# Two-layer diffusion trunk on one core: modulation steps placed in other stages, and a new order around the second layer's first tile of seven products

## The chip, the cores and the metric

The kernel runs on one core of one Trainium2 chip. The metric is device time in microseconds (us). Before the change the median of three runs is 1700.57 us (1700.29 to 1706.34).

Five engines of the core work side by side, each with its own list of instructions: TensorE (PE, matrix products, with its weight loads shown as PEld), VectorE (DVE), ScalarE (ACT), GpSimd (POOL) and SyncE (SP, which in this kernel only issues transfers from memory). An engine works through its list in order, so an instruction that waits holds up those behind it on the same engine. Matrix products go to PSUM, everything else lies in SBUF; a buffer is a slot of a named tile, and a new tile of that name waits until the slot is free.

## The reference, cut to what matters

The model is a trunk of two layers for two groups of tokens that share the weights: 512 sample tokens and 128 prompt tokens, D = 1024 features, float32. Every layer does this for each group:

```python
mod = silu(c) @ w_mod[l] + b_mod[l]          # six parts of 1024 for each group
h = rmsnorm(x, norm_mix) * (1 + mod[1]) + mod[0]
x = x + mod[2] * (mixer(h) @ w_out)
h = rmsnorm(x, norm_ffn) * (1 + mod[4]) + mod[3]
u = conv3(h @ w_up) + conv_b                 # 2 * 2816 columns, three taps along the tokens
x = x + mod[5] * ((silu(u[gate]) * u[a]) @ w_down)
```

The mixer of layer 0 is a latent attention of twelve heads (queries through a rank of 384, keys and values through one of 256, with a positional part of 32) beside a mean over windows of several widths. That of layer 1 is a neighbourhood attention and a windowed attention. At the end `x` is normalised once more. The latents, keys and values of the prompt are outputs too.

`w_mod` is the largest weight that has only two vectors to multiply (the `c` of the sample and that of the prompt): 2 x 1024 x 6144 numbers.

## The kernel before

**Columns and precision.** Activations are held transposed: 128 features on the partitions, tokens along the free side. The 512 sample tokens, a column of zero on either side of the prompt and the 128 prompt tokens make 642 columns. They are worked in two halves: `HALF` is 352 and 290 columns, and the second layer's feed-forward uses `EVEN`, twice 322. A float32 factor is split into a high and a low part of a shorter type, and a product is the sum of high times high, high times low and low times high. So every weight tile and every activation needs a split: ACT writes the high part (L117 for weights) and DVE or POOL subtracts it from the source for the low part (L113).

**Modulation steps.** Most of `w_mod` isn't multiplied on PE. A *step* takes one tile of 128 rows and 512 or 256 columns (`mods_of` lists them, L280): it is loaded (`mod_loads`, L289), and for each of the two vectors it is multiplied by one factor per row and added to an accumulator (`mod_step`, L297). The first vector is done by one instruction of DVE (L316), the second by a product on ACT (L313) and an addition on POOL (L314); in the first of eight steps ACT writes both accumulators (L310). After eight steps DVE transposes each accumulator (L325) and reduces it (L326). When a whole part of 1024 columns is complete, `mod_finish` (L331) makes small products on PE (L337) and the bias on DVE. `mods` makes one step and lets `mod_finish` follow five steps later; `mods_until` stops ahead of a named part. How many raw tiles can be in flight is the `ring`; the queue of the loads is ACT's in the first layer's input projections and SP's later.

Before the change the first layer's parts are distributed so: part 2 (the gate of the mixer) as 16 steps of 512 columns in the input projections, part 4 (the scale of the feed-forward) as 32 steps of 256 in the attention, part 3 (the shift) as 16 steps of 512 in the output projection, two behind each of its products (`MODS_OUT`); part 5 and all of the second layer's parts lie in the first feed-forward, with a ring of two.

**Orders written by hand.** In the start, the input projections, the attention units, the second layer's mixer and all of `Mix` the order of the program is the order of each engine (`manual_schedule`). `MLA_IN` (L49) is a list of pieces of the input projections, each a local function of `mla_in` (L556): `p` a product, `zc` its copy, `sq` squares, `nw` the root of the normalisation by Newton steps, `sc` the scaling with the high part, `lo` the low part, `xc` the copy of the pooled half into a padded tile, `xa`, `xb`, `xm` its sums, `m` one modulation step. `MLA_UNITS` (L63) does the same for an attention unit: one head and one half of the tokens, 24 units in all; the second list is for odd units. `m` there works from the third unit on, until `MLA_MODS` steps are done.

**The output projection of layer 0** (`out_proj`, L450) and the first feed-forward are ordered by the framework's planner, from the order of the program, the readiness of operands and the release of slots; so is SP's queue everywhere. In `out_proj` the loop runs over both halves and eight products: `x` and `w_out` of a product are loaded in the iteration that uses them, three raw `w_out` tiles having been fetched before; behind every product stand the residual sum (`add_x`), the squares and two modulation steps. The normalisation of the first half (`normed`) stands behind product 1 of the second half. It makes `nt` (L424), the high part on ACT (L437) and the low part on DVE (L438) of the activation `ha`, which the feed-forward's first product reads.

**The second layer's feed-forward** is the class `Mix` (L1542). `begin` makes the output projection, the squares, the root and the normalised activations. Its loop over the second half's products has behind each product a piece `after[p_]` (splits of weights for the first tiles, loads, normalisation). The first four tiles of `w_up` (`PLAIN = 4`) are plain: four quarter products, `a` and gate, for two halves. From tile 4 on each tile takes seven products of quarters in place of eight (`p1` to `p7`, L1937) of sums of weights (`sums`, on POOL, gives the blocks S1 to S4; L1897) with sums of activations (T1 to T4). The results are put together on DVE: `u2`, `u3`, `c22`, `c21`, `c12` (L1966 is the addition of all of them). `block` (L1909) splits one block of the weights; `load` (L1892) brings one raw tile into a ring of three, two loads ahead. The convolution of the tile before stands between the products: `gid`/`aid` (centre, ACT), `tapg`/`tapa` (two outer taps, DVE, L1997), `silu`, `mul` (L2020), `ghi`/`glo` (the split of the result). `middle` (L1843) makes the plain tile 3 and the blocks of tile 4, and `slot` (L2029) makes one tile of seven products and the parts of `w_down` that go with it; only the first call, for tile 4, gets the convolution of the tile before (`pv`), since a later tile convolves itself.

Of the kernel before, what the change touches and what calls it, by code (L numbers as in the profile page):

```python
# [49 lines left out]
f.xp0 ln.c f.wk f.xp1 nw.c.0 m nw.c.1 p.q0.1 p.q1.0 zc.q0 sq.q0 sc.c.1.0 p.q1.1 sc.c.1.1 lo.c.1.1 sc.c.0.1 r.wk p.q2.0 sc.c.0.0 rc  # L50
# [15 lines left out]
sc.0 sc.1 pm.0 tu.0 lo.0 v0.1 tu.1 we.2 ou ex.0 wl.0 no.0 ex.1 v0.0 q tu.2 lo.1 no.1 wl.1 lo.2 we.0 m k ke we.1 v pa ve pm.1 qs  # L66
"""]
MLA_MODS = 32
# [21 lines left out]
class Trunk:  # L90
# [359 lines left out]
    def out_proj(self, pool, l, oT, xsrc, after, early=()):  # L450

        nc = self.nc
        x, w, h, normed = [], [], self.acts(), None
        with self.pool(f"wout{l}") as wpool:
            for half in range(2):
                acc = None
                for j in range(KT):
                    if not half:
                        xt = self.T(pool, "x", [P, W], F32, 8)
                        nc.sync.dma_start(xt, xsrc[:, j, :])  # L460
                        x.append(xt)
                        split = early[j] if j < len(early) else self.fetch(self.i["w_out"][l, j], D, *(() if j < 3 else (wpool, ("wo", "wo"), 10)))
                        w.append(split(nc.gpsimd if j in OUT_LO[l] else nc.vector))
# [6 lines left out]
                    if j == 1 and normed:  # L470
                        normed()
# [320 lines left out]
    def mla(self, pool, oT, wq):  # L792
# [663 lines left out]
    def run(self):  # L1456
        tc, nc, i, o = self.tc, self.nc, self.i, self.o
        with ExitStack() as st:
# [38 lines left out]
            self.todo = deque(self.mods_of(0, (2,), 512) + self.mods_of(0, (4,), 256) + self.mods_of(0, (3, 5), 512))  # L1497
            oT = self.acts()
            with self.pool("mla") as pool:
# [5 lines left out]
                with self.psums(mla), self.pool("mla_att") as self.ap:  # L1505
# [36 lines left out]
class Mix:  # L1542
# [122 lines left out]
    def begin(self, po, oT, xsrc, early):  # L1665
# [114 lines left out]
        for p_, j in enumerate((3, 4, 5, 6, 7, 1, 2, 0)):  # L1780
# [6 lines left out]
            after[p_]()  # L1787
# [55 lines left out]
    def middle(self):  # L1843
# [3 lines left out]
        self.sums(4, 0)  # L1847
# [4 lines left out]
        tag(0, "tapg", "silu"), block("S2"), tag(1, "glo"), tag(0, "aid")  # L1852
        self.ca[3], self.cg[3] = self.pair(self.pm, "ca", 3), self.pair(self.pm, "cg", 3)
# [175 lines left out]
    def slot(self, f, pv, nx, downs):  # L2029
# [17 lines left out]
        if nx is None:  # L2047
            self.last_loads(range(0, 6, 2))
# [8 lines left out]
        for d in downs[:1]:  # L2057
            self.parts_d(*d)
# [268 lines left out]
```

## Time and profile before

| what | value |
|---|---|
| runs | 1700.57 us median, 1700.29 and 1706.34 the others |
| profiled execution | 1703.3 us, its span 1701.5 us |
| mean granted clock of PE | 0.972 |
| busy in the span | PE 1584.5, DVE 1260.4, ACT 929.0, POOL 770.5 us |
| start, 0 to 62 us | PE 51.25, DVE 36.42 |
| input projections, 62 to 142 us | PE 64.14, DVE 70.29 of 80 |
| attention units, 142 to 353.6 us | PE 179.51, DVE 159.20, ACT 142.93, POOL 133.18 of 211.6 |
| output projection, 353.6 to 426 us | PE 64.13 of 72.4 |
| first feed-forward, 426 to 925 us | PE 485.92 of 499 |
| second mixer, 925 to 1167 us | PE 230.31 of 242 |
| second output projection and plain tiles, 1167 to 1291 us | PE 121.33 of 124 |
| first tile of seven products, 1291 to 1312 us | PE 12.07 of 21 |
| the other tiles, 1312 to 1646 us | PE 333.78 of 334 |
| end, 1646 to 1701.5 us | PE 42.09 of 55.5 |

The stages are read off the profile's windows; a number behind an engine is its busy time in the stage. The profiled execution is one execution on the chip; its time is the span from the first to the last instruction and a little around it. "Busy" is time in which an instruction of the engine runs. The granted clock is the share of PE's full clock that the chip allowed; where it is lower, the same product takes longer.

### The profile page before, as it was taken

To read this page: it belongs to the slowest core of one execution; us is meant where nothing else is said; L and a number is where in the kernel's file an instruction comes from. 1 tells how busy PE (TensorE), PEld (TensorE's weight loads), DVE (VectorE), ACT (ScalarE), POOL (GpSimd) and SP (SyncE) were. 2 spreads that over 40 slices of the span, in tenths; PEclk is the share of its full clock that TensorE was granted. 3 is DMA by queue.
4 is the path that set the end of the run, shared out by engine and by line. 5 is a ranking of instruction groups with operands and counts; after the bars stand their busy time and mean duration, and the time that the engine had idled before them with its cause. 6 is when DMAs were issued, how large, how long until landed. Compare 5 with 4: busy or idle time off the path is not lost.

```text
span 1701.5 us, 28135 instructions
## 1 busy us (share of the span) xinstructions
PE 1584.5 (93%) x10349; PEld 1512.7 (89%) x10349; DVE 1260.4 (74%) x2190; ACT 929.0 (55%) x1792; POOL 770.5 (45%) x704
## 2 busy tenths in 40 slices
PE   8878888889999999999997999998997999999996
PEld 2777777788899999999997999987997999999996
DVE  4896788768999778977638777776687666776766
ACT  3554777655555345544345678886565344444445
POOL 2154777554234332534063234663325456555543
PEclk9997999998999999999999999998999999999999
DMA  9431212044344444544225211114222122222221
GB/s 342 137 100 56 63 50 80 14 160 140 112 143 151 159 137 139 159 142 137 84 86 183 70 42 58 53 43 163 75 82 85 63 89 88 78 78 74 78 73 63
DMA packets 79032, 175.62 MB, mean 103 GB/s; under 512 B 11598, under 2 KB 29342, under 8 KB 78894
## 3 DMA queue, kind: packets, MB, share of 16 engines
q1 hardware_dynamic: 76398, 169.55, 30.9%
q10 hardware_dynamic: 2304, 4.20, 0.8%
q8 instruction: 82, 1.34, 0.3%
q14 instruction: 56, 0.46, 0.1%
q0 software_dynamic: 192, 0.07, 0.0%
HBM read 166.71 MB, written 8.03 MB: 103 GB/s over the span
## 4 chain that ended last, share of the span: by engine, by line
PE 49%; DVE 16%; issue 6%; ACT 5%; DMA 5%; POOL 1%; SPq 0%; DVEq 0%; ACTq 0%; POOLq 0%
PE p L1594 24%; PE mm L137 19%; DMA mraw<-in_w_mod_dram 4%; DVE wlo L113 2%; DVE acc L316 2%; PE sc L1209 1%; PE tr L1247 1%; PE o L1259 1%; DVE u L511 1%; DVE nt L424 1%; ACT whi L117 1%; DVE ha L438 1%; DVE g L113 1%; DVE v L1997 1%; ACT mt L313 1%
## 5 line engine op out<-in xcount | busy, mean ns | idle before, releaser
L314 POOL TENSOR_TENSOR acc<-acc,mt 128x512 f32<-128x512 f32 x115 | 175.5, 1526 | 266.1 <-ACT mt L313 251.3
L137 PE MATMUL mm<-ha,whi 128*128 128x352 f32 (+1 forms) x1168 | 287.5, 328 | 4.7 <-ACT ha L437 4.6
L137 PE MATMUL mm<-hb,whi 128*128 128x290 f32 (+1 forms) x1168 | 244.2, 302 | 1.1 <-ACT hb L437 1.1
L137 PEld LDWEIGHTS mm<-ha,whi 128*128 128x128 f32 (+1 forms) x1168 | 202.4, 190 | 6.5 <-ACT ha L437 4.7
L316 DVE SCALAR_TENSOR_TENSOR acc<-mraw,cs,acc 128x512 f32<-128x512 f32 (+1 forms) x165 | 169.7, 1035 | 47.5 <-DMA mraw<-in_w_mod_dram 45.9
L137 PEld LDWEIGHTS mm<-hb,whi 128*128 128x128 f32 (+1 forms) x1168 | 192.8, 191 | 4.0 <-issue 2.7
L137 PE MATMUL mm<-ha,wlo 128*128 128x352 f32 (+1 forms) x584 | 188.9, 324 | 0.0
L113 POOL TENSOR_TENSOR wlo<-raw,whi 128x1024 fp32r<-128x1024 f32 (+3 forms) x46 | 98.3, 2142 | 175.1 <-ACT whi L117 116.3
L137 PE MATMUL mm<-hb,wlo 128*128 128x290 f32 (+1 forms) x584 | 174.7, 299 | 0.0
L113 POOL TENSOR_TENSOR w<-raw,w 128x512 fp32r<-128x512 f32 (+1 forms) x68 | 90.3, 1339 | 172.9 <-ACT w L117 164.8
L137 PE MATMUL mm<-g,whi 128*128 128x352 f32 (+1 forms) x704 | 157.8, 311 | 7.0 <-DVE x L447 5.2
L117 ACT CAST whi<-raw 128x1024 fp32r<-128x1024 f32 (+3 forms) x117 | 116.0, 996 | 68.5 <-PE mm L137 52.0
L313 ACT ACTIVATE mt<-mraw,cs 128x512 f32<-128x512 f32 x115 | 81.7, 720 | 113.4 <-DMA mraw<-in_w_mod_dram 101.0
L1594 PE MATMUL p<-g,d 128*128 128x320 f32 (+1 forms) x912 | 140.0, 312 | 0.9 <-POOL d L113 0.9
L1594 PEld LDWEIGHTS p<-g,d 128*128 128x128 f32 x912 | 136.4, 189 | 2.3 <-POOL d L113 2.1
L1594 PE MATMUL p<-hb,w 128*128 128x322 f32 (+1 forms) x816 | 129.0, 313 | 7.4 <-DVE cg L1966 6.7
L1594 PEld LDWEIGHTS p<-hb,w 128*128 128x128 f32 x816 | 123.4, 191 | 8.3 <-DVE cg L1966 6.9
L137 PEld LDWEIGHTS mm<-g,whi 128*128 128x128 f32 x704 | 118.4, 189 | 9.5 <-ACT ha L437 3.9
L1594 PE MATMUL p<-ha,w 128*128 128x322 f32 x768 | 122.7, 314 | 1.5 <-ACT ca L1960 1.5
L1594 PEld LDWEIGHTS p<-ha,w 128*128 128x128 f32 x768 | 117.5, 192 | 1.9 <-ACT ca L1960 1.8
L137 PEld LDWEIGHTS mm<-hb,wlo 128*128 128x128 f32 (+1 forms) x584 | 112.5, 193 | 0.0
L137 PEld LDWEIGHTS mm<-ha,wlo 128*128 128x128 f32 (+1 forms) x584 | 110.1, 188 | 0.5
(332 smaller groups left out, 3763.1 us busy)
## 6 DMA issues: line engine op xcount, KB each, us to landing
raw<-in_w_up_dram SPq DMA_DIRECT2D x90, 512.0 KB, 3.6
mraw<-in_w_mod_dram SPq DMA_DIRECT2D x128, 256.0 KB, 2.9
raw<-in_w_out_dram SPq DMA_DIRECT2D x19, 512.0 KB, 4.0
raw<-in_w_in_odd_dram SPq DMA_DIRECT2D x18, 512.0 KB, 3.6
mraw<-in_w_mod_dram SPq DMA_DIRECT2D x16, 512.0 KB, 8.8
raw<-in_w_down_dram SPq DMA_DIRECT2D x16, 512.0 KB, 3.6
draw<-in_w_down_dram SPq DMA_DIRECT2D x40, 192.0 KB, 2.4
raw<-in_w_down_dram SPq DMA_DIRECT2D x16, 384.0 KB, 3.1
```

What stands on the lines that cost most here:

```text
L113: (engine or self.nc.vector).tensor_sub(lo, src, Fv(hi))
L117: self.nc.scalar.copy(hi, src)
L137: self.pe = self.nc.tensor.matmul(out, lhsT=l, rhs=r, start=k == 0, stop=k == n - 1)
L313: nc.scalar.activation(t, raw, AF.Copy, scale=s)
L314: nc.gpsimd.tensor_add(acc, acc, t)
L316: nc.vector.scalar_tensor_tensor(out=acc, in0=raw, scalar=s, in1=acc, op0=ALU.mult, op1=ALU.add)
L424: self.nc.vector.scalar_tensor_tensor(out=t[:, c], in0=x[k][:, c0:c1][:, c], scalar=self.mod[l][:, ma, k, v : v + 1], in1=rs[:, c], op0=AL ...
L438: nc.vector.scalar_tensor_tensor(out=lo[:, c], in0=t[:, c], scalar=ss, in1=Fv(hi[:, c]), op0=ALU.add, op1=ALU.subtract)
L511: nc.vector.scalar_tensor_tensor(out=u[:, 1:W], in0=ps[:, 0 : W - 1], scalar=cw[:, j, 0:1], in1=u[:, 1:W], op0=ALU.mult, op1=ALU.add)
L1209: nc.tensor.matmul(ps[:, c : c + n], lhsT=u.Q[:, a], rhs=x[e], start=e == 0, stop=e == 1)
L1247: nc.tensor.transpose(tp[:, j * P : (j + 1) * P], u.p[b][:, x : x + P], self.ident)
L1594: self.t.pe = self.nc.tensor.matmul(ps[:, 0:n], lhsT=l_, rhs=r[:, 0:n], start=first and m == 0, stop=last and m == count - 1, skip_group_c ...
```

## The change

1. **Input projections.** The last eight `m` leave `MLA_IN`, so that eight of sixteen stay. `nw.q.1` goes behind `lo.q.0.2`, and `xc.1` comes ahead of that `lo`.
2. **Attention.** The second half of part 2 is now 16 steps of 256 columns ahead of part 4; an odd unit has two `m` in place of one, and `MLA_MODS` goes from 32 to 48. The two fixed calls of `mod_finish` (ahead of the third unit, behind the last) are gone, so that only the count of five steps calls it.
3. **Output projection of layer 0.** `x` is loaded two tiles ahead, raw `w_out` three ahead, the ring of raw modulation tiles goes from two to four (in the feed-forward too), and the first half's normalisation stands behind product 2 instead of 1. `out_proj` has only this one caller.
4. **Second layer, `begin`.** The pieces `after[6]` and `after[7]` (two splits of weights and two loads) stand behind the loop instead of in it.
5. **Second layer, `middle` and the first `slot`.** `load("a", 5)`, the block A12 and `load("g", 5)` come earlier in `middle`; S1 comes ahead of `mul`; the first product of tile 4 and its copy move from the slot into `middle`. In tile 4's slot `tapg` and `silu` come ahead of `p6`; `tapa` and `p5` come ahead of `mul`, S2 and S3; `c22` follows `p5` directly; the parts of `w_down` come behind S3. The other slots keep their order.

```diff
@@ MLA_IN
-f.xp0 ln.c f.wk f.xp1 nw.c.0 m nw.c.1 p.q0.1 ...
+f.xp0 ln.c f.wk f.xp1 nw.c.0 nw.c.1 p.q0.1 ...
-lo.c.0.0 zc.q1 lo.c.0.1 sq.q1 lo.c.1.0 m.d r.xp0 kp.1 kp.0 ke.1 p.q2.1 f.wq m.d r.xp1 f.wv ke.0 xz m zc.q2 p.xp0.0 m sq.q2 m sm.q p.xp0.1
-ln.q r.wv nw.q.0 xc.0 xa.0 sc.q.0.0 p.xp1.0 r.wq p.xp1.1 iv.0 sc.q.0.1 xb.0 lo.q.0.0 sc.q.0.2 lo.q.0.1 nw.q.1 lo.q.0.2 m.d xm.0 sc.q.1.0
-sc.q.1.1 xc.1 lo.q.1.0 sc.q.1.2 lo.q.1.1 xa.1 lo.q.1.2 xb.1 iv.1 m.d xm.1
+lo.c.0.0 zc.q1 lo.c.0.1 sq.q1 lo.c.1.0 r.xp0 kp.1 kp.0 ke.1 p.q2.1 f.wq r.xp1 f.wv ke.0 xz zc.q2 p.xp0.0 sq.q2 sm.q p.xp0.1
+ln.q r.wv nw.q.0 xc.0 xa.0 sc.q.0.0 p.xp1.0 r.wq p.xp1.1 iv.0 sc.q.0.1 xb.0 lo.q.0.0 sc.q.0.2 lo.q.0.1 xc.1 lo.q.0.2 nw.q.1 xm.0 sc.q.1.0
+sc.q.1.1 lo.q.1.0 sc.q.1.2 lo.q.1.1 xa.1 lo.q.1.2 xb.1 iv.1 xm.1
@@ MLA_UNITS, odd units
-... lo.2 we.0 m k ke we.1 v pa ve pm.1 qs
+... lo.2 we.0 m m k ke we.1 v pa ve pm.1 qs
-MLA_MODS = 32
+MLA_MODS = 48
@@ out_proj
+        def load_x():
+            if len(x) < KT:
+                x.append(self.T(pool, "x", [P, W], F32, 8))
+                nc.sync.dma_start(x[-1], xsrc[:, len(x) - 1, :])
+        for _ in range(2):
+            load_x()
...
-                        xt = self.T(pool, "x", [P, W], F32, 8)
-                        nc.sync.dma_start(xt, xsrc[:, j, :])
-                        x.append(xt)
-                        split = early[j] if j < len(early) else self.fetch(...)
-                        w.append(split(nc.gpsimd if j in OUT_LO[l] else nc.vector))
+                        load_x()
+                        w.append(raws[j](nc.gpsimd if j in OUT_LO[l] else nc.vector))
+                        if len(raws) < KT:
+                            raws.append(self.fetch(self.i["w_out"][l, len(raws)], D, wpool, ("wo", "wo"), 10))
...
-                    if j == 1 and normed:
+                    if j == 2 and normed:
@@ mla, run
-            if t == 2:
-                self.mod_finish("tr")
...
-            self.todo = deque(self.mods_of(0, (2,), 512) + self.mods_of(0, (4,), 256) + ...)
+            self.todo = deque(self.mods_of(0, (2,), 512)[:KT] + self.mods_of(0, (2,), 256)[2 * KT :] + self.mods_of(0, (4,), 256) + ...)
...
-                        self.mod_finish("tr")
...
-                self.mods_in(pool, len(self.todo), 2, nc.sync)
+                self.mods_in(pool, len(self.todo), 4, nc.sync)
@@ Mix.begin
-            after[p_]()
+            if p_ < 6:
+                after[p_]()
+        after[6](), after[7]()
@@ Mix.middle
-        self.sums(4, 0)
+        self.sums(4, 0), self.load("a", 5)
...
+        block("A12"), self.load("g", 5)
...
-        tag(0, "mul", "ghi"), block("S1")
+        block("S1"), tag(0, "mul", "ghi")
         self.plain(3, 1, 1, 1)
-        tag(0, "glo")
+        self.p1(4)
         self.copy(3, 0, 1)
-        block("A12"), self.load("a", 5)
-        self.copy(3, 1, 1), self.gid(3)
-        block("A22", "S4"), self.load("g", 5)
+        tag(0, "glo")
+        self.copy(3, 1, 1), self.copy1(4), self.gid(3)
+        block("A22", "S4")
@@ Mix.slot, for tile 4 alone
+            sums(0), conv("tapg", "silu")
+            self.p6(f)
+            self.u2(f), sums(1), conv("aid"), block("A11")
+            self.p7(f)
+            self.u3(f), conv("tapa")
+            self.p5(f)
+            self.c22(f), conv("mul"), block("S2", "S3")
+            for d in downs[:1]:
+                self.parts_d(*d)
+            for d in downs[2:3]:
+                self.load_d(*d)
+            conv("ghi", "glo"), block("S1")
```

More of the change, by code (lines that the diff above doesn't have):

```diff
@@ L65 @@
 """, """
-sc.0 sc.1 pm.0 tu.0 lo.0 v0.1 tu.1 we.2 ou ex.0 wl.0 no.0 ex.1 v0.0 q tu.2 lo.1 no.1 wl.1 lo.2 we.0 m k ke we.1 v pa ve pm.1 qs
+sc.0 sc.1 pm.0 tu.0 lo.0 v0.1 tu.1 we.2 ou ex.0 wl.0 no.0 ex.1 v0.0 q tu.2 lo.1 no.1 wl.1 lo.2 we.0 m m k ke we.1 v pa ve pm.1 qs
 """]
-MLA_MODS = 32
+MLA_MODS = 48
 ODD_NA = ["""
@@ L452, in out_proj @@
         nc = self.nc
-        x, w, h, normed = [], [], self.acts(), None
+        x, w, h, normed, raws = [], [], self.acts(), None, list(early)
+        def load_x():
[4 more added lines that the diff above has]
+            load_x()
         with self.pool(f"wout{l}") as wpool:
@@ L1496, in run @@
             nc.vector.tensor_scalar(out=self.nsink, in0=self.sink, scalar1=-1.0, scalar2=None, op0=ALU.mult)
-            self.todo = deque(self.mods_of(0, (2,), 512) + self.mods_of(0, (4,), 256) + self.mods_of(0, (3, 5), 512))
+            self.todo = deque(self.mods_of(0, (2,), 512)[:KT] + self.mods_of(0, (2,), 256)[2 * KT :] + self.mods_of(0, (4,), 256) + self.mods_of(0, (3, 5), 512))
             oT = self.acts()
@@ L1857, in middle @@
         self.copy(3, 1, 0)
-        tag(0, "mul", "ghi"), block("S1")
+        block("S1"), tag(0, "mul", "ghi")
         self.plain(3, 1, 1, 1)
+        self.p1(4)
+        self.copy(3, 0, 1)
         tag(0, "glo")
-        self.copy(3, 0, 1)
-        block("A12"), self.load("a", 5)
-        self.copy(3, 1, 1), self.gid(3)
-        block("A22", "S4"), self.load("g", 5)
+        self.copy(3, 1, 1), self.copy1(4), self.gid(3)
+        block("A22", "S4")
         for c, (f0, f1) in enumerate(self.CHUNKS[1:]):
@@ L2046, in slot @@
             self.load_d(*d)
-        if nx is None:
-            self.last_loads(range(0, 6, 2))
-        self.p1(f)
-        sums(0), block("A11"), conv("tapg")
-        self.copy1(f)
-        conv("silu")
-        self.p6(f)
-        self.u2(f), sums(1), conv("aid")
-        self.p7(f)
-        self.u3(f), block("S2"), conv("tapa", "mul"), block("S3")
-        for d in downs[:1]:
-            self.parts_d(*d)
-        for d in downs[2:3]:
-            self.load_d(*d)
-        self.p5(f)
-        self.c22(f), conv("ghi", "glo"), block("S1")
+        if pv is None:
+            if nx is None:
+                self.last_loads(range(0, 6, 2))
+            self.p1(f)
+            sums(0), block("A11")
+            self.copy1(f)
+            self.p6(f)
+            self.u2(f), sums(1)
+            self.p7(f)
+            self.u3(f), block("S2", "S3")
+            for d in downs[:1]:
[3 more added lines that the diff above has]
+            self.p5(f)
+            self.c22(f), block("S1")
+        else:
+            sums(0), conv("tapg", "silu")
+            self.p6(f)
+            self.u2(f), sums(1), conv("aid"), block("A11")
+            self.p7(f)
+            self.u3(f), conv("tapa")
+            self.p5(f)
+            self.c22(f), conv("mul"), block("S2", "S3")
+            for d in downs[:1]:
+                self.parts_d(*d)
+            for d in downs[2:3]:
+                self.load_d(*d)
+            conv("ghi", "glo"), block("S1")
         if nx is None:
```

3 lines of the change are left out of this document (1 added, 2 removed).

## The prediction

> **What bounds the kernel now.** First the page's head, then the stages one by one.
>
> ```profile
> PE 1584.5 (93%) x10349; PEld 1512.7 (89%) x10349; DVE 1260.4 (74%) x2190; ACT 929.0 (55%) x1792; POOL 770.5 (45%) x704
> ```
>
> TensorE (PE) sets the time: busy for 1584.5 of the 1701.5 us of the span. A change can win only where PE stands still or loses its clock, so I looked at the stages that the diff touches, in the view that cuts the span into windows. A row gives start:end and length, then the busy time of PE, of its weight loads, of VectorE (DVE), ScalarE (ACT) and GpSimd (POOL), the granted clock, the DMA share and GB/s. The stages are: the end of the input projections; attention units 2 to 17; units 18 and 19; units 20 and 21; a piece of the first layer's feed-forward; the second layer's first seven-product tile.
>
> ```profile
> 83.00:142.00 59.00, 45.60 (x259) 43.08 (x259) 52.27 (x71) 27.26 (x54) 33.70 (x31) 0.83 0.38 114
> 165.46:308.80 143.34, 121.60 (x837) 109.88 (x835) 114.33 (x241) 103.65 (x245) 103.64 (x104) 0.99 0.18 58
> 308.80:328.13 19.33, 16.15 (x103) 14.53 (x103) 14.50 (x31) 10.86 (x25) 7.04 (x7) 0.91 0.08 28
> 328.13:339.91 11.78, 10.08 (x71) 9.01 (x71) 8.82 (x20) 7.93 (x21) 6.99 (x8) 1.00 0.01 1
> 625.00:735.00 110.00, 109.46 (x746) 108.99 (x744) 95.86 (x102) 58.48 (x78) 41.38 (x28) 1.00 0.46 147
> 1288.00:1315.50 27.50, 18.35 (x106) 16.80 (x106) 18.95 (x26) 17.41 (x31) 13.14 (x10) 0.88 0.17 52
> ```
>
> In the first row DVE is the full engine (52.27 of 59) and PE is at 45.60; in the feed-forward PE is full, so nothing done there shows; in the last row PE misses 9.15 us. Who PE waited for in the first of these stages, in the output projection (353 to 440 us) and around the start of the second layer's feed-forward (1200 to 1320 us) is in the view of waits (total, times, longest):
>
> ```profile
> PE tr L137 <- ACT px L683: 4.8, 1, 4.8
> PE b L359 <- DVE sqz L404: 3.4, 2, 2.8
> PE tr L137 <- DVE q L774: 3.0, 1, 3.0
> PE tr L137 <- DVE qan L113: 1.9, 1, 1.9
> ...
> PE b L337 <- DVE mred L326: 4.2, 1, 4.2
> PE mm L137 <- DVE wo L113: 3.5, 1, 3.5
> ...
> PE p L1594 <- DVE cg L1966: 6.7, 1, 6.7
> PE v L359 <- ACT sq L1614: 2.7, 1, 2.7
> PE p L1594 <- ACT ca L1960: 1.5, 1, 1.5
> ```
>
> **Part 1, eight modulation steps leave the input projections.** They are the last eight of sixteen, with 512 columns each. What they cost DVE from 83 us on, and where the last two lie, in the groups by form and in DVE's timeline (start, length):
>
> ```profile
> L316 DVE SCALAR_TENSOR_TENSOR acc<-mraw,cs,acc 128x512 f32<-128x512 f32 x11 | 15.1, 1402 | 0.0
> ...
> 118.57 1.34 DVE L378 TENSOR_TENSOR r<-r 128x290 f32<-128x290 f32 x1
> ...
> 122.47 3.50 DVE L316 SCALAR_TENSOR_TENSOR acc<-mraw,cs,acc 128x512 f32<-128x512 f32 x2
> 125.89 0.94 DVE L627 SCALAR_TENSOR_TENSOR z<-z,gq,r 128x290 f32<-128x290 f32 x2
> ...
> 129.56 3.46 DVE L316 SCALAR_TENSOR_TENSOR acc<-mraw,cs,acc 128x512 f32<-128x512 f32 x2
> 132.94 0.70 DVE L325 STREAM_TRANSPOSE mt<-acc 128x512 f32<-128x512 f32 x1
> ...
> 135.61 0.52 DVE L774 TENSOR_TENSOR q<-tr,qtab 128x352 f32<-128x352 f32 x1
> ```
>
> The eleven accumulations are 15.1 us; the two transposes and two reductions between 132.94 and 135.61 add some 2.7 (135.61 − 132.94). So 17.8 us leave an engine that is 89% full, and they lie right ahead of what PE waits for: 122.47 to 125.89 in front of the second half's query normalisation, 129.56 to 135.61 in front of the product that frees a PSUM tile (L774). PE's four waits sum to 13.1 us (4.8 + 3.4 + 3.0 + 1.9). Moving `nw.q.1` (four instructions from 118.57) behind `lo.q.0.2` and `xc.1` ahead serves the same waits. Not all of it goes: after the first half's queries PE still has to wait for `nw.q.1` and the chain from 125.89 to 129.56, at most 3.9 (122.47 − 118.57) and 3.7 (129.56 − 125.89), of which a part lies behind PE's first-half products; I leave 3 us standing (an estimate), late in place of the old waits. The granted 0.83 should recover about 1 us. **Gain 11 us**; at least 6 (129.56 to 135.61 stands directly ahead of a wait), at most 14. ACT also issues eight fewer loads there.
>
> **Part 2, sixteen steps of 256 columns enter the attention.** Each has one accumulation on DVE, one product on ACT and one addition on POOL; the first of each eight has two ACT instructions instead, the last has two transposes and two reductions that wait for POOL. The rows, and from the view of the tile `acc` the spread (min/median/max in ns) and DVE's waits; the last is the steps' loads:
>
> ```profile
> L316 DVE SCALAR_TENSOR_TENSOR acc<-mraw,cs,acc 128x256 f32<-128x256 f32 x28 | 25.7, 918 | 0.3
> ...
> L316 DVE SCALAR_TENSOR_TENSOR acc<-mraw,cs,acc x28: 458/696/1617, 168.1 to 303.3; 128x256 f32<-128x256 f32 x28
> L325 DVE STREAM_TRANSPOSE mraw<-acc x8: 445/445/447, 200.3 to 307.1; 128x256 f32<-128x256 f32 x8
> ...
>   POOL acc L314: 8.1, 4
> ...
> mraw<-in_w_mod_dram SPq DMA_DIRECT2D x29, 128.0 KB, 2.2
> ```
>
> On DVE: 14 × 0.918 = 12.9, eight transposes and reductions at about 0.44 = 3.5, two more waits at 8.1/4 = 4.0; together 20.4 us. That is the upper bound (all of it on the path). The lower: units 2 to 17, with 32 steps, leave PE unbusy for 21.74 us, 1.36 a unit; units 20 and 21, with none, 0.85 a unit. The difference, 0.51 for two steps, gives 0.25 a step and 4 us for sixteen. Between them: of the sixteen, eight fall in units 2 to 17 (one more each in the odd units) and eight in units 18 to 20. In the latter DVE would have 23.3 + 10.2 = 33.5 us of work in 31.1 us, so at least 2.4 must show there, and the others displace an ACT or POOL instruction that PE needs somewhat more often than now. I take **a loss of 7 us**, nearer the lower row. Sixteen loads of 128 KB on the SP queue, 2.2 us each to land, three in flight, take the place of eight on ACT's; SP's other loads there are the weights, needed units later. The modulations' two small products on PE move from fixed places to the count of five steps after the last one: as many as before.
>
> [...]
>
> **Part 3, the output projection.** Loads (four modulation tiles in flight, x two ahead, weights three ahead) and the half's normalisation one product later. PE's waits of 3.5 (a split of `wo` behind an accumulation that waited for its load) and 4.2 (the shift's reduction) are 7.7 us. DVE's wait for those loads, the clock after the second stop, and the normalisation of the first half:
>
> ```profile
> DVE acc L316 <- DMA mraw<-in_w_mod_dram: 8.2, 7, 2.5
> ...
> 397.30:409.13 11.83, 7.64 (x37) 6.91 (x36) 9.49 (x15) 8.48 (x12) 6.06 (x4) 0.71 0.50 165
> 409.13:425.43 16.30, 16.30 (x122) 16.07 (x120) 16.10 (x33) 8.20 (x15) 4.27 (x17) 1.00 0.18 59
> ...
> 415.46 1.07 DVE L424 SCALAR_TENSOR_TENSOR nt<-x,mod,r 128x352 f32<-128x352 f32 x2
> ...
> 425.29 0.57 DVE L438 SCALAR_TENSOR_TENSOR ha<-nt,mod,ha 128x352 fp32r<-128x352 f32 x1
> ```
>
> At 0.71 of the clock for some 6 us after the stop, about 1.7 us come back too: 9.4. The price: `ha` is finished at 425.86, and the window's end at 425.43 is that of the projection, with the feed-forward's first product next. One product later in the program (16.30/5 = 3.3 us) with a stop of 4.2 us gone means that the sums run about as late against the start of the half, while its end comes sooner. That wait can be nothing (DVE's 8.2 us of waits are gone, and the products take `ha` one by one) or 5 us (3.3 and the 1.7); I take 2. **Gain 7.4**, from 3 to 9.4. In the feed-forward four tiles in flight change nothing: PE is full (109.46 of 110).
>
> **Part 4, two splits behind the last square.** `after[6]` and `after[7]` go behind the loop. DVE and PE around the wait of 2.7 us:
>
> ```profile
> 1231.71 2.36 DVE L113 TENSOR_TENSOR w<-raw,w 128x512 fp32r<-128x512 f32 x2 [1.06 <-ACT w L117]
> ```
>
> The last residual sum stands behind that split in the program; it can run 3.4 us sooner (the two splits' 2.36 and their 1.06). The four splits still precede the root on DVE. **Gain 2** of 2.7; zero to 2.7.
>
> **Part 5, the first seven-product tile.** PE's 6.7 us end with `cg` (L1966, the read of S1's product). What DVE does ahead of it, and the loads on SP:
>
> ```profile
> 1306.88 1.21 DVE L113 TENSOR_TENSOR w<-s,w 128x512 fp32r<-128x512 f32 x1 [1.98 <-ACT w L117]
> ...
> 1309.85 0.83 DVE L2020 TENSOR_TENSOR va<-v,cg 128x642 f32<-128x642 f32 x1
> 1310.60 1.17 DVE L113 TENSOR_TENSOR d<-draw,d 128x512 fp32r<-128x512 f32 x1
> 1311.68 0.48 DVE L1966 TENSOR_TENSOR cg<-p,cg 128x322 f32<-128x322 f32 x1
> ...
> 1268.46 11.55 SPq L1895 DMA_DIRECT2D raw<-in_w_up_dram  x3
> ...
> 1299.79 2.21 SPq L1895 DMA_DIRECT2D raw<-in_w_up_dram  x2
> ```
>
> The new order puts `cg` ahead of the block S2 (1.21 and its wait of 1.98), the product `va` (0.83) and `d` (1.17): 5.2 us less in front of it. The split of A12 comes ahead of it now. The third load of the first SP row is already a of tile 5, so the line that moves it does nothing; g of tile 5 (1299.79) follows A12. **Gain 4.5**: 5.2 less 0.7, since `d` is late next. At least 1.5 (the wait for `ca`), at most 8.2.
>
> **The sum.** −11 + 7 − 7.4 − 2 − 4.5 = −17.9 us. The profiled execution took 1703.3 us, 1701.5 of them its span: 1685.4. It stands 2.7 above the median of the three runs, 1700.57; against that the forecast is **1683 us**.
>
> **The rivals.**
> - *The moved steps show in full in the attention.* For it: DVE is at 80% there, the maximum of 1617 ns. Against it: the 0.25 a step. 20.4 in place of 7: 1696 us.
> - *They hide.* 4 lost, 9.4 at the output projection, 2.7 and 6 in the second layer, 11 at first: −25, 1675 us.
> - *The wait for `ha` takes the output projection's gain.* A new stop at the feed-forward's start: 1690 us.
> - *The reordering does not do what it says*: the tile's stop goes from `cg` to `d` or A22 and only 1.5 is left: 1686 us.
> [...]
>
> **How the numbers follow.** Forecast 0.48; steps in full 0.20; hidden 0.13; `ha` 0.09; order without effect 0.05; slower 0.05. The forecast's own bounds are 1676 to 1690. The range goes from 1671 (4 below hidden) to 1699 (3 above the steps in full). This kernel's measurement tells 0.5% (8.5 us) from no change: faster means below 1692. Forecast, hidden, `ha` and the order lie below it, 0.75; steps in full and most of the slower case, whose price is 1706, lie inside, and 0.04 of that case is left for sums above 1709: faster 0.75, same 0.21, slower 0.04.
>
> **What would show it.** The first score product starts about 11 us sooner, without waits on `px` and `q`. Attention from unit 2 to the first output product takes about 7 us more. PE no longer waits for `wo` and `mred`; a wait on `ha` would be the price. At the second layer's root the 2.7 is gone, and 6.7 shrinks to 2 or 3. It is wrong if attention grows by over 15 us, or if `mred` or `wo` still stop PE.

## The result and the profile after

The changed kernel takes 1731.2 us, median of five runs (1730.89 to 1732.51), against 1703.14 us for the kernel before (five runs): a ratio of 1.0174, 95% interval 1.0161 to 1.0188. It is 28 us slower. The forecast was 1683 us, 17.9 us faster by its own sum, and the time lies outside its range.

I first cut both profiled executions at the same events: start of the input projections, first score product, first output product, first product of the feed-forward, first score product of the second layer, and around its first seven-product tile. These are windows of the kernel before (start:end, length, busy time of PE, its weight loads, DVE, ACT, POOL, then granted clock, DMA share, GB/s):

```profile
62.00:141.82 79.82, 63.96 (x378) 60.48 (x376) 70.11 (x90) 36.50 (x70) 40.91 (x34) 0.87 0.45 135
141.82:353.63 211.81, 179.72 (x1200) 162.86 (x1199) 159.38 (x338) 143.08 (x339) 133.18 (x135) 0.96 0.13 43
353.63:426.67 73.04, 64.48 (x399) 63.10 (x398) 56.92 (x87) 38.10 (x61) 40.29 (x43) 0.91 0.52 174
426.67:955.60 528.93, 515.24 (x3441) 507.84 (x3439) 412.90 (x527) 258.18 (x370) 186.57 (x140) 0.99 0.43 135
...
1231.00:1326.18 95.18, 83.37 (x526) 80.98 (x525) 74.49 (x115) 57.07 (x115) 42.85 (x31) 0.95 0.25 81
```

And the same stretches of the kernel after:

```profile
62.00:133.80 71.80, 60.68 (x379) 57.41 (x378) 56.75 (x75) 33.41 (x65) 36.03 (x31) 0.93 0.43 125
133.80:376.66 242.86, 188.61 (x1201) 172.19 (x1199) 181.58 (x360) 151.47 (x357) 145.62 (x149) 0.91 0.14 44
376.66:456.98 80.32, 64.55 (x398) 62.80 (x398) 76.08 (x93) 42.49 (x68) 51.14 (x50) 0.93 0.55 185
456.98:983.18 526.20, 513.68 (x3441) 507.45 (x3439) 413.02 (x521) 254.61 (x362) 184.83 (x133) 0.99 0.41 131
...
1258.62:1354.00 95.38, 86.08 (x527) 83.64 (x526) 75.47 (x114) 57.06 (x115) 41.64 (x31) 0.93 0.25 81
```

| stage | before | after | difference | forecast |
|---|---|---|---|---|
| input projections | 79.82 | 71.80 | −8.0 | −11 |
| attention | 211.81 | 242.86 | **+31.1** | +7 |
| output projection | 73.04 | 80.32 | **+7.3** | −7.4 |
| feed-forward | 528.93 | 526.20 | −2.7 | 0 |
| root and first seven-product tile | 95.18 | 95.38 | +0.2 | −6.5 |

The spans differ by 27.7 us (1729.2 and 1701.5), and the column adds up to that within 0.2. Most of the loss lies in the attention, and it is in two parts: PE without work grew from 32.1 to 54.3 us, and the same products took 188.6 instead of 179.7 us because the granted clock fell from 0.96 to 0.91.

Who PE waits for after the change, in the view of waits of the whole kernel (total, times, longest; the rows with L846 and the one with `sc` and `kh` are the attention's):

```profile
PE tr L846 <- DVE pt L850: 19.0, 13, 4.8
PE sc L137 <- ACT kh L117: 12.2, 5, 5.5
PE mm L137 <- DVE x L447: 8.9, 6, 2.0
PE b L359 <- DVE sq L404: 7.3, 2, 5.8
...
PE tr L846 <- DVE kl L113: 4.9, 3, 2.0
PE tr L137 <- ACT qan L636: 4.8, 1, 4.8
...
PE mm L137 <- DVE wo L113: 4.6, 1, 4.6
PE p L1598 <- DVE cg L1973: 3.3, 1, 3.3
...
PE tr L137 <- DVE qan L113: 3.3, 3, 2.1
PE p L1598 <- ACT w L117: 2.8, 1, 2.8
...
PE p L1598 <- DVE d L113: 1.4, 2, 1.0
PE p L1598 <- ACT d L117: 1.1, 1, 1.1
```

And what the other engines wait for inside the attention, first after the change, then before:

```profile
ACT mraw L313 <- DVE acc L316: 18.8, 20, 2.1
DVE mraw L325 <- POOL acc L314: 14.3, 6, 4.5
...
PE sc L137 <- ACT kh L117: 12.2, 5, 5.5
ACT acc L310 <- DVE mraw L325: 8.2, 6, 4.4
```

```profile
PE tr L839 <- DVE pt L843: 13.3, 12, 3.4
...
ACT mraw L313 <- DVE acc L316: 8.3, 11, 1.0
DVE mraw L325 <- POOL acc L314: 8.1, 4, 2.2
...
ACT acc L310 <- DVE mraw L325: 4.1, 6, 1.1
...
PE sc L137 <- ACT kh L117: 1.5, 3, 0.7
```

PE's time without work grew by 22.2 us. The waits for `kh` have 10.7 of it (12.2 and 1.5) and those for `pt` at L846 5.7 (19.0 and 13.3); the rest is spread over smaller rows.

How such a wait is made shows in one odd unit of the kernel after, in the timeline (start, length, engine):

```profile
250.49 0.31 PE L137 MATMUL sc<-kh,q 128*128 128x320 f32 x1
250.56 0.39 POOL L837 TENSOR_TENSOR pp<-pp,s 128x128 f32<-128x128 f32 x1
250.91 2.33 POOL L113 TENSOR_TENSOR wlo<-raw,whi 128x1024 fp32r<-128x1024 f32 x1
253.21 0.72 POOL L314 TENSOR_TENSOR acc<-acc,mraw 128x256 f32<-128x256 f32 x1
...
253.96 0.45 DVE L325 STREAM_TRANSPOSE mraw<-acc 128x256 f32<-128x256 f32 x1 [4.48 <-POOL acc L314]
...
254.44 0.51 ACT L310 ACTIVATE acc<-mraw,cs 128x256 f32<-128x256 f32 x1 [4.37 <-DVE mraw L325]
...
255.85 0.35 ACT L117 CAST kh<-tr 64x256 fp32r<-64x256 f32 x1
...
256.25 0.64 PE L137 MATMUL sc<-kh,q 128*128 128x320 f32 x1 [5.45 <-ACT kh L117]
```

A step here is an eighth one. POOL has a unit's normalisation (L837) and a weight split (`wlo`) ahead of the step's addition (L314). DVE's transpose waits 4.48 us for that addition. The second step of the pair is the first of the next eight: ACT has to write the accumulator that DVE is still to transpose, and waits 4.37 us. Behind it on ACT stands the keys' split `kh`, and PE waits 5.45 us for that. Three engines stand still in turn for one addition that nothing on PE needs yet. This is the longest of the six eighth steps: the other five waits of DVE are 1.5 to 2.6 us.

### The profile page after: what moved, and what is told of

Read it like the earlier page. It is cut to its first block, busy times and chain, and to the rows that moved or that the text cites. A ratio compares the mean times of both kernels' runs of the same rounds, so it can differ in the third digit from the quotient of the medians.

```text
span 1729.2 us, 28212 instructions
## 1 busy us (share of the span) xinstructions
PE 1590.7 (92%) x10349; PEld 1520.8 (88%) x10349; DVE 1289.7 (75%) x2197; ACT 935.0 (54%) x1805; POOL 785.3 (45%) x715
## 4 chain that ended last, share of the span: by engine, by line
PE 59%; DVE 9%; issue 6%; ACT 3%; POOL 2%; DMA 0%; DVEq 0%; POOLq 0%; ACTq 0%
PE mm L137 28%; PE p L1598 24%; DVE acc L316 2%; PE sc L1214 1%; PE tr L1252 1%; PE o L1264 1%; DVE nt L424 1%; DVE ha L438 1%; POOL w L113 1%; DVE x L447 1%; DVE sq L404 1%; DVE pt L113 0%; ACT whi L117 0%; DVE q L1054 0%; DVE p L1225 0%
## 5 line engine op out<-in xcount | busy, mean ns | idle before, releaser
L314 POOL TENSOR_TENSOR acc<-acc,mt 128x512 f32<-128x512 f32 x112 | 180.9, 1615 | 266.9 <-ACT mt L313 242.9
L316 DVE SCALAR_TENSOR_TENSOR acc<-mraw,cs,acc 128x512 f32<-128x512 f32 (+1 forms) x168 | 187.6, 1122 | 12.8 <-DMA mraw<-in_w_mod_dram 9.1
L113 DVE TENSOR_TENSOR wlo<-raw,whi 128x1024 fp32r<-128x1024 f32 x71 | 97.6, 1375 | 23.2 <-ACT whi L117 22.4
```

What stands on the lines that cost most here:

```text
L113: (engine or self.nc.vector).tensor_sub(lo, src, Fv(hi))
L314: nc.gpsimd.tensor_add(acc, acc, t)
L316: nc.vector.scalar_tensor_tensor(out=acc, in0=raw, scalar=s, in1=acc, op0=ALU.mult, op1=ALU.add)
```

## The experiments

Each run was timed against the kernel before on the same chip, whose median was 1702.3 to 1703.3 us in the five sets.

**The change in three.** The first two parts alone (input projections and attention):

```diff
 MLA_IN, MLA_UNITS, MLA_MODS, todo, mod_finish: as in the change
```

> The kernel before with the first two parts of the change alone: eight modulation steps leave the input projections, sixteen of 256 columns enter the attention. Theory A (the whole loss is made here): the traces show the first score product 8.0 us sooner and the stretch from it to the output projection 31.0 us longer (242.9 in place of 211.8), so 23 us slower than the kernel before. Rival B (the attention is only that slow together with the later loads and the other parts of the change): the forecast's own sum, -11 + 7, so 4 us faster.

Measured: 1723.97 us, ratio 1.0134 (1.0117 to 1.0151), so 21 us slower; the attention takes 242.3 us in its trace. Theory A holds: most of the loss is made here, without the other parts.

The third part alone:

```diff
 out_proj: as in the change
-                self.mods_in(pool, len(self.todo), 2, nc.sync)
+                self.mods_in(pool, len(self.todo), 4, nc.sync)
```

> The kernel before with the third part alone: loads ahead, four raw modulation tiles in flight, the first half's normalisation one product later. Theory A (with four tiles in flight more modulation steps run in the output projection, 23 accumulations in place of 17 on VectorE, which is then full): the stage 7 us longer, of which the feed-forward gives 3 back, so about 4 us slower. Rival B (the stage is slow only because the attention ends late and hands it work): 7.4 us faster, as forecast.

Measured: 1708.68 us, ratio 1.0042 (1.0027 to 1.0057), 5 us slower: nearer to theory A. The groups on DVE in the output projection, before (first fence) and with this part (second):

```profile
L316 DVE SCALAR_TENSOR_TENSOR acc<-mraw,cs,acc 128x512 f32<-128x512 f32 x17 | 18.3, 1077 | 6.6 <-DMA mraw<-in_w_mod_dram 6.5
L404 DVE TENSOR_TENSOR sq<-sq,sq 128x352 f32<-128x352 f32 x7 | 5.1, 731 | 1.6 <-ACT sq L402 1.5
```

```profile
L316 DVE SCALAR_TENSOR_TENSOR acc<-mraw,cs,acc 128x512 f32<-128x512 f32 x21 | 29.7, 1414 | 0.2
L404 DVE TENSOR_TENSOR sq<-sq,sq 128x352 f32<-128x352 f32 x7 | 9.1, 1303 | 0.6 <-ACT sq L402 0.6
```

DVE no longer waits for a load (6.5 us before, none now), and that is what fills it: 21 accumulations instead of 17, each a third longer, 11.4 us more in all, so the residual sums and squares that PE needs come late.

The fourth and fifth part alone:

```diff
 Mix.begin, Mix.middle, Mix.slot: as in the change
```

> The kernel before with the fourth and fifth part alone, both in the second layer. By the trace of the changed kernel the time from the second layer's first output product to the last product is the same as before (521.6 against 521.5 us): no difference. By the forecast (2 and 4.5 us): 6.5 us faster.

Measured: 1700.12 us, ratio 0.9988 (0.9973 to 1.0004): not to be told from no change. The three medians add up to 23 us of the 28. In the traces both of the first two runs get about 3 us back in the feed-forward (525.98 and 525.77 us against 528.93), and the whole change only 2.7 once; why it gets them back was not tried.

**The attention.** The transposes of an eighth step issued two steps later, with two sets of accumulators and, since the raw tile is gone by then, into a tile of their own:

```diff
-            self.acc = [self.T(pool, f"acc{v}", [P, n]) for v in range(2)]
+            self.acc = [self.T(pool, f"acc{v}", [P, n], F32, 2 if mode == "i" else 1) for v in range(2)]
...
+        if mode == "i":
+            self.due = (self.tick + 2, l, m, c, n, self.acc)
+        else:
+            self.mod_rows(l, m, c, n, self.acc)
...
-            tr = raw if mode == "i" else self.T(pool, "mt", [P, n], F32, 2)
-            nc.vector.transpose(tr, self.acc[v])
+            tr = self.T(pool, "mt", [P, n], F32, 2)
+            nc.vector.transpose(tr, acc[v])
```

> As the run with the first two parts alone, but in the attention the transposes and reductions that follow an eighth step are issued two steps later, from accumulators of which there are two sets, so that VectorE doesn't wait for GpSimd's last addition and ScalarE's first step of the next eight doesn't wait for the transposes. All work stays. Theory C (those waits, 14.3 us on VectorE and 8.2 on ScalarE in the trace, are what stops TensorE): 14 to 20 us faster than without it. Rival D (VectorE and GpSimd have too much to do in these units, and shut each other out): at most 4 us faster.

Measured: 1708.82 us, ratio 1.0041 (1.0028 to 1.0054), 15 us faster than without it; theory C. DVE's waits for POOL's additions (14.3 us in the changed kernel, 13.1 in the run without the late transposes) are gone. What is left shows in the window of its attention, in the waits there and in one unit of its timeline, in this order:

```profile
133.41:358.17 224.76, 181.03 (x1201) 164.44 (x1199) 177.01 (x360) 149.84 (x357) 144.59 (x149) 0.95 0.15 47
```

```profile
PE sc L139 <- ACT kh L119: 13.1, 5, 6.8
ACT mraw L315 <- DVE acc L318: 12.8, 11, 2.8
```

```profile
280.14 5.81 POOL L115 TENSOR_TENSOR wlo<-raw,whi 128x1024 fp32r<-128x1024 f32 x2
...
281.51 4.71 DVE L318 SCALAR_TENSOR_TENSOR acc<-mraw,cs,acc 128x256 f32<-128x256 f32 x2
283.82 0.51 ACT L315 ACTIVATE mraw<-mraw,cs 128x256 f32<-128x256 f32 x1 [2.85 <-DVE acc L318]
...
286.31 0.51 ACT L315 ACTIVATE mraw<-mraw,cs 128x256 f32<-128x256 f32 x1 [1.98 <-DVE acc L318]
286.72 0.35 ACT L119 CAST kh<-tr 64x256 fp32r<-64x256 f32 x1
...
287.12 0.63 PE L139 MATMUL sc<-kh,q 128*128 128x320 f32 x1 [6.79 <-ACT kh L119]
```

Two accumulations take 4.71 us beside two splits on POOL (458 ns is the shortest single one in the kernel before). ACT writes its product over the raw tile, so it must wait until DVE has read it; `kh` stands behind.

The two steps of an odd unit put behind the keys' split:

```diff
-... lo.2 we.0 m m k ke we.1 v pa ve pm.1 qs
+... lo.2 we.0 k ke m we.1 v pa ve m pm.1 qs
```

> The run with the late transposes (1708.8 us), and in the odd attention units the two modulation steps no longer stand together ahead of the keys' product and split, but behind them, one behind the split and one behind the values' split. Theory E (ScalarE's in-place product of a step waits for VectorE's accumulation, which waits for a split on GpSimd, and the keys' split behind it makes TensorE wait: 6.8 us in one unit, 13.1 us in all odd units): 6 to 12 us faster, 1697 to 1703. Rival F (the work of the steps on VectorE sets the units, wherever they stand): within 2 us of 1708.8.

Measured: 1706.88 us, ratio 1.0027 (1.0013 to 1.0041): within 2 us, rival F by its number. The stretch is 224.4 us as against 224.8; PE's waits went from `kh` to other operands, and ACT's waits for DVE's accumulations grew from 12.8 to 16.4 us. Moving the steps within the unit moves the wait and doesn't remove it. F's reason, the work itself, is not shown by this; the run with a tile of its own below speaks against it.

The kernel before, its 32 steps, with the late transposes alone:

```diff
 MLA_IN, MLA_UNITS, MLA_MODS, todo: as before
+        if mode == "i":
+            self.due = (self.tick + 2, l, m, c, n, self.acc)
```

> The kernel before with its 32 steps in the attention, and only the transposes and reductions of the four eighth steps two steps later, from two sets of accumulators. Theory C: VectorE's waits of 8.1 us for GpSimd go, 3 to 6 us faster than before. Rival: before the change these steps fall at a place of the unit that costs TensorE nothing, within 2 us.

Measured: 1695.89 us, ratio 0.9961 (0.9948 to 0.9974), 6.5 us faster. That is theory C, a little above its range. The kernel before paid for the same wait, with four eighth steps instead of six: its attention falls from 211.8 to 205.1 us.

Eight steps less in the input projections, late transposes, and the sixteen steps in units 18 to 23:

```diff
-... we.0 k m m pm.0 pa lo.2 ...
+... we.0 k m m pm.0 mx pa lo.2 ...
-... we.0 m k ke we.1 v pa ve pm.1 qs
+... we.0 m k ke mx we.1 mx v pa ve pm.1 mx qs
+                elif name == "mx" and t in (20, 21):
+                    self.mods("tr", 1, "i")
```

> Eight steps out of the input projections and sixteen of 256 columns into the attention as in the change, with the late transposes, but units 2 to 17 keep the order and the 32 steps of the kernel before, and the sixteen stand in units 18 to 23 (two pairs as before, eight more in units 20 and 21). Theory K (a step costs TensorE what VectorE has no time for in its unit; units 20 to 23 have 4.6 us of work in 6): 5 to 9 us lost in the attention against 13, so 1699 to 1703. Rival F (a step costs 0.8 us wherever it stands): 1707, as in the run with late transposes.

Measured: 1702.51 us, ratio 1.0002 (0.9992 to 1.0012), at the upper end of theory K. The attention takes 217.8 us, 7 less than with the steps in every odd unit.

Two runs leave work out, on top of the late transposes:

```diff
+            elif v == 0 and mode == "i":
+                pass
```

> As the run with late transposes, but in the attention the first vector's accumulations on VectorE (42, some 40 us) are left out, so that its modulations are wrong there. Theory K (VectorE's work sets what is left of the loss): the stretch from the first score product to the output projection 224.8 us becomes 205 to 213. Rival L (GpSimd's additions and ScalarE's products do): still over 218.

```diff
+            elif v and mode == "i":
+                pass
```

> As the run with late transposes, but in the attention the second vector's products on ScalarE and additions on GpSimd (42 each, some 33 us on GpSimd and 21 on ScalarE) are left out, so that its modulations are wrong there. Theory K: the stretch of 224.8 us stays over 218. Rival L: 205 to 213. If VectorE and GpSimd shut each other out, both runs come below 218.

Measured: 1678.81 us, ratio 0.9863 (0.9838 to 0.9888), and 1691.72 us, ratio 0.9939 (0.9915 to 0.9962). The attention takes 195.7 us without DVE's accumulations and 207.3 without POOL's and ACT's share: both below 218, so neither K nor L alone. It is the outcome put down in advance for VectorE and GpSimd shutting each other out. But both runs also cut the chain from DVE through ACT, so only a run that keeps the work can tell the work from the chain:

```diff
-                t = raw if mode == "i" else self.T(pool, "mt", [P, n], F32, 2)
+                t = self.T(pool, "mp", [P, n], F32, 2) if mode == "i" else self.T(pool, "mt", [P, n], F32, 2)
```

> As the run with late transposes (1708.8 us, 224.8 us from the first score product to the output projection), but ScalarE writes the second vector's product to a tile of its own, not over the raw tile, so that it doesn't wait for VectorE's accumulation to have read it (12.8 us of waits). All work stays. Theory M (what is left of the sixteen steps' price is this chain from VectorE through ScalarE): the stretch falls to 212 to 218 us. Theory N (it is the work itself, with VectorE and GpSimd shutting each other out): 222 us or more.

Measured: 1692.78 us, ratio 0.995 (0.9936 to 0.9965), some 15 us faster than the run without it and 9.6 us faster than the kernel before. Theory M, and more than it expected; the window of its attention and PE's longest wait in it:

```profile
133.20:341.53 208.33, 174.83 (x1201) 158.41 (x1199) 174.16 (x360) 147.28 (x357) 145.71 (x149) 0.98 0.17 52
```

```profile
PE sc L139 <- DVE kl L115: 4.6, 4, 3.1
```

Theory N, with all work kept, is refuted as the main cause. PE's wait for `kh` is down to 1.1 us in all and the one for `pt` to 11.3. Loads are no rival: in the attention of the run without the own tile no engine waits for a raw modulation tile.

With all 48 steps the attention now takes 208.3 us, less than the 211.8 of the kernel before with 32, and the clock is at 0.98. With 32 steps and the same two repairs (the second run of the last group below) it takes 204.9:

```profile
141.88:346.79 204.91, 177.89 (x1200) 163.46 (x1199) 163.45 (x338) 140.53 (x339) 133.64 (x135) 0.96 0.14 44
```

The last two runs of the last group have the same 48 steps and both repairs. Their attention takes 208.3 us in one of them (the fourth) and 211.9 in the other:

```profile
133.90:345.76 211.86, 180.02 (x1200) 164.15 (x1199) 174.86 (x360) 147.23 (x357) 145.43 (x149) 0.95 0.17 50
```

So sixteen steps cost 3.4 to 7.0 us (0.2 to 0.4 each) once nothing waits in line, and 31.1 as the change had them. Most of the spread is PE's clock (0.95 to 0.98 for the same instructions). The work is not free: with the first vector's 42 accumulations left out as well, the attention took 195.7 us, another 12.6 us less (0.3 each).

**The input projections alone**, eight steps left out of the kernel:

```diff
 MLA_IN: as in the change
-            self.todo = deque(self.mods_of(0, (2,), 512) + ...)
+            self.todo = deque(self.mods_of(0, (2,), 512)[:KT] + ...)
```

> The first part alone: the input projections in the change's order with eight steps, the other eight left out of the kernel altogether, so that half of the mixer's gate is wrong; the attention and all else as before. By the forecast: 11 us faster than the kernel before. By the traces of the runs with that order (first score product 8.0 to 8.6 us sooner): 8 us faster. If the attention only catches up with what it waits for elsewhere: under 4 us.

Measured: 1696.79 us, ratio 0.9965 (0.9952 to 0.9979), 5.6 us faster. The first score product comes 8.0 us sooner, as in the other runs with that order; the output projection is 2.3 us longer. Its weights are not the reason, since PE's wait for the `wo` split is 3.5 us as before; its wait for the modulation's reduction `mred` is 5.8 us instead of 4.2. Why that one grows was not tried.

**The output projection.** The third part with two raw modulation tiles, and four tiles without the rest of it:

```diff
 out_proj: as in the change
 self.mods_in(pool, len(self.todo), 2, nc.sync)
```

> The third part alone, but with two raw modulation tiles in flight as before: the loads of x and weights ahead and the normalisation one product later stay. Theory G (four tiles in flight let the planner put more steps, 21 accumulations in place of 17 at 1414 instead of 1077 ns, ahead of the residual sums and the normalisation): as fast as the kernel before or up to 4 us faster, 1699 to 1703. Rival H (the later normalisation or the loads make it slow): 1708, as with four.

Measured: 1703.61 us, ratio 1.0011 (0.9998 to 1.0024): as fast as the kernel before, theory G, and rival H is out. DVE makes 18 accumulations of 1081 ns in the stretch.

```diff
-                self.mods_in(pool, len(self.todo), 2, nc.sync)
+                self.mods_in(pool, len(self.todo), 4, nc.sync)
```

> The kernel before with four raw modulation tiles in flight behind the attention, and nothing else. Theory G: 4 to 6 us slower than before, 1707 to 1709. Rival H: no slower than before.

Measured: 1712.59 us, ratio 1.0059 (1.004 to 1.0078), 10 us slower: more than theory G expected. DVE makes 22 accumulations of 1449 ns in the stretch. Without weights loaded ahead PE also waits 12.4 us at once for a split of `wo` (the second row is of the whole kernel; 6.5 us of it lie in this stage):

```profile
PE mm L137 <- ACT wo L117: 12.4, 1, 12.4
PE mm L137 <- DVE x L447: 11.7, 6, 3.9
```

The tiles in flight are the loss, and the rest of the third part takes some 4 us of it back (1712.6 and 1708.7). With two tiles the loads and the later normalisation gain nothing. Why each accumulation takes a third longer with four tiles was not tried.

**The second layer.** The fifth part alone:

```diff
 Mix.begin: as before
 Mix.middle, Mix.slot: as in the change
```

> The fifth part alone (middle and the first tile of seven products), with the two splits behind the last square where they were. Theory I (the moved splits of the fourth part made the new wait of 2.8 us for a weight split in the plain tiles, in place of the 2.7 us that they saved): the 2.7 us wait at the root is back, the 2.8 us wait is gone, and the time is that of both parts together, 0 to 3 us under the kernel before. Rival J (the fourth part gained): 2 to 3 us slower than both together, so no faster than before.

Measured: 1700.78 us, ratio 0.9992 (0.9981 to 1.0003), theory I: the wait at the root is back (2.6 us), the 2.8 us wait for a weight split is gone, and the time is that of both parts.

**Put together.** Late transposes with 32 steps and the second layer's parts; the same with ACT's product in its own tile; then the changed kernel with both repairs, once without its third part and once with that part and two tiles:

```diff
 1: self.due, Mix as in the change
 2: self.due, Mix as in the change, tile "mp"
 3: self.due, Mix as in the change, tile "mp", MLA_IN, MLA_UNITS, MLA_MODS, todo as in the change
 4: as 3, out_proj as in the change, self.mods_in(pool, len(self.todo), 2, nc.sync)
```

> The kernel before with the late transposes for its 32 steps (1695.9 us alone) and the fourth and fifth part of the change. If the second layer's parts gain nothing: 1696. If they gain what the medians of their own run showed (3 us): 1693. By the forecast's 6.5: 1689.

> The run with both (late transposes, the fourth and fifth part, 32 steps), with ScalarE's product in a tile of its own as well. By theory M: 4 to 8 us faster than without it. By theory N: within 2 us of it.

> The changed kernel with both repairs in the attention (transposes of an eighth step two steps later, ScalarE's product in a tile of its own) and without the third part: the output projection as in the kernel before. If the parts add up: 1692.8 less what the second layer's parts give (nothing to 3 us), 1690 to 1693.

> The same with the third part's loads ahead and later normalisation, but two raw modulation tiles in flight. By the run of that part with two tiles (no difference from the kernel before): as fast as the one above, within 3 us. By the forecast's gain at the output projection: 3 to 7 us faster.

Measured: 1693.74 us, ratio 0.9954 (0.9941 to 0.9966); 1697.03 us, 0.9962 (0.9948 to 0.9976); 1694.97 us, 0.995 (0.9934 to 0.9967); 1696.8 us, 0.9963 (0.9949 to 0.9976). The second layer gave between nothing and 3 us, and the third part nothing even here. The own tile gave nothing with 32 steps, where theory M had expected 4 to 8 us: with 32 steps and late transposes alone, ACT waits only 4.8 us for DVE's accumulations (12.8 with 48), and PE 1.3 us for `kh` (13.1), so little of the chain was left to cut; that this is the reason is argued. The intervals of all four, and of the run with the own tile alone, overlap: five kernels that are 5 to 10 us faster than the kernel before by their medians, and none shown to be the best. They also overlap that of the kernel before with late transposes alone (0.9948 to 0.9974). So the late transposes are shown to gain, and that the parts of the change gain anything on top of them is not shown. The gains don't add up, and why not was not tried.

## Why the prediction was wrong, point by point

**Part 2 failed, and with it the sum.** "The difference, 0.51 for two steps, gives 0.25 a step and 4 us for sixteen" took the price of work, and that is about right: with the waits taken away it is 0.2 to 0.4 a step. The term of 7 us was mis-sized all the same, since the stage lost 31.1: what was missing is the order on the engines. The prediction did count two more eighth steps, at "8.1/4 = 4.0" in the upper bound, as time of DVE alone. But five steps a pair of units instead of four move the eighth step from the one step of every second odd unit to five different places in the units. At two of them POOL has more ahead of it (waits of 4.5 and 2.6 us, where 2.2 was the longest before), and in the unit shown DVE's wait becomes ACT's and then PE's. ACT's waits to write over a tile that DVE still has to read grew too, from 8.3 to 18.8 us, and in odd units the keys' split stands behind them. The late transposes gave back 15 us, the own tile some 15 more. The upper bound of 20.4 us was no bound: it summed one engine's work, while the loss of 31.1 comes for the most part from a chain over three engines, and 8.9 of it is products that took longer at the lower clock. The prediction's own sign of being wrong, an attention longer by over 15 us, came.

**The rivals** "steps in full" (1696) and "slower" (1706) had the right place, and both were priced as DVE's time, so both were too small. The slower one named the wrong mechanism: its price, 30.2 us (14 × 1.617 and the 3.5 and 4.0 of Part 2), put all 14 accumulations at the longest time of the trace, as if each stood behind POOL as long. Such waits show, but they are older than the change: in the kernel before, of the 28 accumulations between 160 and 310 us, the 14 that began beside a POOL instruction with 0.6 us or more of it left took 0.91 to 1.62 us, and the other 14, with 0.11 us of one left or none, 0.46 to 0.49; after the late transposes two took the 4.71 us beside 5.81 us of splits above. But no run shows the longest time for all of them: over the attention the accumulation's mean went from 918 to 1017 ns only, 4.2 us for 42 of them, and the run with the own tile has the same work on both engines. Without POOL's additions DVE is still busy 173.1 us, as against 177.0.

**Part 1**: −11 forecast, −8.0 in the trace, −5.6 in the end. The waits on `px` (4.8) and `q` (3.0) went, as the text said it would show. But "I leave 3 us standing" was too little: the chain from `nw.q.1` stops PE for 4.8 (`qan`, ACT) and 3.3 us (`qan`, DVE, 1.9 before) in its place. PE without work fell from 15.9 to 11.1 us, and the clock (0.87 to 0.93) gave another 3.3 where 1 was put.

**Part 3**: −7.4 forecast, +7.3 measured. The step that failed is "DVE's 8.2 us of waits are gone" as a gain. They went, but of PE's two waits only `mred` (4.2 us) did: `wo`, which was to go too, stops PE for 4.6 us instead of 3.5. The waits for loads had been what held the modulation steps back, and the planner, which takes what is ready, put four more of them (and slower ones) ahead of work that PE waits for. The `ha` rival had the right kind of cause but the wrong tile: the new stop of 5.8 us is on the squares. That the loads ahead would win by themselves is not borne out either (two tiles: no difference).

**Parts 4 and 5**: −6.5 forecast, +0.2 in the stage. Both mechanisms came as told: the 2.7 us at the root are gone and 6.7 became 3.3. The price was left out. Part 4's splits are now late for the plain tiles (2.8 us for `w`), and `d` costs 1.4 and 1.1 us where 0.7 was put. PE without work fell from 11.8 to 9.3 us only, and its products took 2.7 us longer at a clock of 0.93 instead of 0.95. In the run of 1693.7 us the second layer from its first output product to its last product took 515.6 us in the trace, as against 521.1 in the one with late transposes alone, and the 2.8 us for `w` were not there; the medians differ by 2.2 us only. Which of the two happens, and why, stays open.

## What to carry to other kernels

Before adding off-path work to a tuned stretch, follow each new instruction's operands over the in-order engines: what stands ahead of its producer, and what stands behind its consumer. The price here was the chain far more than the work (31.1 us as the change had the steps, 3.4 to 7.0 once nothing waits in line), so the cure was to consume a result later, which paid in the kernel before as well, and to give a product a buffer of its own, which paid only with the 48 steps. And a wait for a load can be what keeps off-path work out of the way: here four raw modulation tiles in place of two let 22 accumulations into the output projection where 17 had been, in a run 10 us slower than the kernel before.

## What the runs showed of the hardware that was not expected

In the attention PE lost time in two ways at once. The same 1200 products took 179.7 us at a granted clock of 0.96 in the kernel before, and 188.6 at 0.91 after, while PE's time without work grew from 32.1 to 54.3 us. More time without work and a lower clock come together in these two rows; that the one brings the other is not shown, since no run here varied the length of one stop alone.

The stops don't settle the clock in these runs. Two kernels with the same instructions in the attention (the own tile, and the third of the last group) have PE without work for 33.5 and 31.8 us there, and longest waits of 3.1 and 3.2 us, but the clock was 0.98 in one and 0.95 in the other, and the same products took 174.8 and 180.0 us. The stretch took 208.3 and 211.9 us, so 3.5 us of difference came without any change of the order there; what decides it stays open.
